# A hybrid attention and mLSTM layer on one core: log-sigmoid on token rows, attention stacks put together by DMA moves, two mLSTM evictions on ScalarE

## The chip, the cores and the metric

The kernel runs on one core of one Trainium2 chip. The metric is the time of one execution in microseconds on the device (us). In the profile PE is TensorE, PEld its weight loads, DVE is VectorE, ACT is ScalarE, POOL is GpSimd and SP is SyncE, whose work here is to issue DMAs. The engines run beside each other; each takes its own instructions strictly in the order in which the program lists them.

## The reference

One decoder layer over 1024 tokens of width 1024 in float32. The mixer projects the normalised input once and feeds two groups of heads, 8 attention heads of width 64 and 4 mLSTM heads of width 128; a gated feed-forward network with a short convolution follows.

```python
def _hybrid_mixer(h, w_in, ...):
    proj = h @ w_in
    aq, ak, av, mq, mk, mv, mo, mig, mfg = jnp.split(proj, SPLITS, axis=-1)
    att = _dilated_attention(att_heads(aq), att_heads(ak), att_heads(av))
    att = _rmsnorm(...)
    mqk = jax.nn.silu(_causal_dwconv(jnp.concatenate([mq, mk], axis=-1), mlstm_conv_w, mlstm_conv_b))
    ...
    log_i = (mig + mlstm_i_bias)
    log_f = jax.nn.log_sigmoid((mfg + mlstm_f_bias))
    hm = _mlstm_chunkwise(ml_heads(mq), ml_heads(mk) * (MLSTM_HEAD_DIM ** -0.5), ml_heads(mv), log_i, log_f)
    hm = jax.nn.sigmoid(mo) * _rmsnorm(...)
    return jnp.concatenate([att, hm], axis=-1) @ w_out

def _conv_ffn(h, w_ffn_up, ffn_conv_w, ffn_conv_b, w_ffn_down):
    gate, val = jnp.split(_causal_dwconv(h @ w_ffn_up, ffn_conv_w, ffn_conv_b), 2, axis=-1)
    return (jax.nn.silu(gate) * val) @ w_ffn_down
```

The attention scores are `q @ k.T`, 64 wide, over three dilated bands. In mLSTM the running sums of `log_f` and the running maxima over `log_f` and `log_i` give each token its weights.

## The kernel before

**Products in three parts.** A float32 operand is split into a rounded part and the rest (names with `h` and `l`: `xh`, `xl`, `w5h`, `w5l`), and a product is made of three matmuls of these parts (`mm3`, lines 315 to 318). ACT copies the first part, DVE or POOL subtracts it to get the second.

**The order.** Every stage is a generator, a lane with a priority. A planner (`Lanes.run`, lines 184 to 207) goes on with the first lane in order of priority whose tiles are ready by a model of the engines' clocks (`Clock`, lines 30 to 142). So the list of every engine is fixed when the program is built, and a change of one stage moves the instructions of others. Tiles of 128 x 1040 words are taken from 48 pages (`page`, `free`) and eight PSUM banks (`bank`, `freebank`); a lane that finds none free waits.

**The stages.** The projections run from the start to about 450 us in the order `m3 g0 g1 v0 m4 m5 v1 m6 m7 a0 h0 h1 h2 h3 a1 h4 h5 h6 h7` (line 392): `m` and `h` are the q and k rows of mLSTM and of attention heads, `g` the output gate with the eight i and f gate columns, `v` and `a` the values. Matmuls of mLSTM and attention are put between them. From about 450 us follow the output projection and, from about 625 us to the end, the feed-forward network, in which seven products take the place of eight by sums of blocks. These sums of weights are made by large DMAs from DRAM to DRAM (`sums`, lines 772 to 791): four pairs of a copy, issued by ACT, and an adding DMA, issued by POOL, of 5632 KB each into `usum` while the mixer runs, and later four pairs into `tsum`. All other DMAs are issued by SP, in one order, and SP waits in that order.

**The gates** (lines 696 to 767). `gn` holds the gate columns, 128 tokens x 8 tiles x 8. Sixteen transposes on PE turn them into rows `li` and `gz` of 4 x 1024, ACT evicts these with the bias; DVE and ACT make the log-sigmoid on the 4 x 1024 rows, DVE two scans, and from them `rows`, which PE transposes back (line 751) for all four mLSTM heads.

**mLSTM** (lines 794 to 890). For each half of a head four blocks: `ET` (decay weights), `ST` (weighted scores), `pk` (transposed k, multiplied by the last column of `ET`), and per block one PSUM bank with three products, whose first is copied to `nm` and whose second is added to it.

**Attention stacks** (lines 896 to 922). `t` holds q of one head on partitions 0 to 63 and k on 64 to 127. The scores need 128 partitions with both parts of both: `q1` is [first part; rest] and `q2` [rest; first part] of q, `kS` [rest; first part] of k. They are made by four copies and two subtractions of 64 partitions each, which move data between the halves as they go (in the trace `q` is both `q1` and `q2`). `copy` (lines 306 to 313) gives each copy to ACT or DVE, whichever is free first by the model.

Of the kernel before, what the change touches and what calls it, by code (L numbers as in the profile page):

```python
# [8 lines left out]
F32 = mybir.dt.float32  # L9
# [13 lines left out]
NBANK = 8  # L23
PGW = 1040

P_XN, P_FN, P_CW, P_CB, P_AW, P_MW, P_FW, P_FB, P_IB, P_FBI, P_N = (
    0, 8, 16, 48, 56, 60, 64, 64 + 132, 64 + 132 + 44, 64 + 132 + 45, 64 + 132 + 46)


class Clock:  # L30
# [187 lines left out]
def need(*tiles, pg=0, bk=0, cond=None, keep=0, kb=0):  # L218

    return tiles, pg, bk, cond, keep, kb  # L220
# [3 lines left out]
def tile_hybrid_layer(ctx, tc, xT, x, w_t, w_v, w_g, w_o, w_uq, w_dq, params, fnw, c_id, c_att, c_sel,  # L224
# [77 lines left out]

    def f32(ap):
        return ap.bitcast(F32)

    def copy(out_, in_, scale=None):

        if clk.eng.get("act", 0.0) <= clk.eng.get("dve", 0.0):
            act.activation(out_, in_, AF.Copy, **({} if scale is None else {"scale": scale}))
        elif scale is None:  # L310
            dve.tensor_copy(out_, in_)
        else:
            dve.tensor_scalar(out_, in_, scale, None, op0=OP.mult)
# [380 lines left out]
    G = {}  # L694

    def gates():
        yield need(pg=9, bk=1, cond=lambda: ("g", 1) in flags)
        rows_pg, urow_pg = page("rows"), page("urow", F32R)
        rows, urow = rows_pg[0:68, :S], urow_pg[0:64, :S]
        pool.memset(rows, 0.0)  # L700
        act.activation(urow, rows[0:64], AF.Copy)
        tmp = [page(n) for n in ("li", "gz", "lf", "ge", "gu", "gt", "uu")]
        li, z, lf, e, u, t, uu = [p[0:4, :S] for p in tmp]
        for hf in range(2):
            sl = slice(hf * 512, (hf + 1) * 512)
            for g, dst, b in ((0, li, P_IB), (1, z, P_FBI)):
                yield need(gn, bk=1)
                p = bank("pgt")
                for i in range(4):
                    pe.transpose(p[0:4, i * 128:(i + 1) * 128], gn[:, hf * 4 + i, g * 4:g * 4 + 4], ident)  # L710
                act.activation(dst[:, sl], p[0:4, :], AF.Identity, bias=pr[0:4, b:b + 1])
                freebank(p)
        yield need(z)
        dve.scalar_tensor_tensor(e, z, -1.0, z, op0=OP.mult, op1=OP.min)
        yield need(e)
        act.activation(e, e, AF.Exp)
        yield need(e)
        dve.tensor_scalar(u, e, 1.0, None, op0=OP.add)
        yield need(u)
        act.activation(lf, u, AF.Ln)  # L720
        dve.tensor_scalar(t, u, 1.0, None, op0=OP.subtract)
        dve.tensor_sub(t, e, t)
        dve.reciprocal(u, u)
        yield need(u)
        dve.tensor_mul(t, t, u)
        dve.tensor_add(lf, lf, t)
        dve.scalar_tensor_tensor(lf, z, 0.0, lf, op0=OP.min, op1=OP.subtract)
        yield need(lf)
        b, m = u, e
        dve.tensor_tensor_scan(b, rst, lf, 0.0, op0=OP.mult, op1=OP.add)  # L730
        dve.tensor_tensor_scan(m, lf, li, 0.0, op0=OP.add, op1=OP.max)
        yield need(m)
        dve.tensor_sub(uu, b, m)
        dve.tensor_sub(rows[0:4, :], li, b)
        yield need(rows)
        dve.tensor_scalar(rows[64:68, :], m, -41.0, None, op0=OP.max)
        act.activation(urow[0:4, :], uu, AF.Copy)
        dve.tensor_copy(rows[32:36, 0:128], uu[:, 0:128])
        u3 = uu.rearrange("p (c t) -> p c t", t=128)
        m3 = m.rearrange("p (c t) -> p c t", t=128)  # L740
        dve.tensor_tensor(rows[32:36, 128:].rearrange("p (c t) -> p c t", t=128), u3[:, 1:8, :],
                          m3[:, 0:7, 127:128].to_broadcast([4, 7, 128]), op=OP.add)
        dve.tensor_sub(urow[32:36, :], uu, f32(urow[0:4, :]))
        free(*tmp)
# [12 lines left out]
        yield need(rows, bk=1)
        p = bank("pdec")
        for h in range(4):
            pe.matmul(p[:, h * 8:(h + 1) * 8], sel[32:36, h * 128:(h + 1) * 128],  # L760
                      rows[32:36, 127:1024:128], start=True, stop=True)
        act.activation(dec.rearrange("p h c -> p (h c)"), p[:, :32], AF.Exp)
        freebank(p)
        free(rows_pg)
        G["urow"] = urow
        G["pg"] = urow_pg
        free(rst_pg, sel_pg)
# [26 lines left out]
    def mlstm(h):  # L794
# [8 lines left out]
        for hf in range(2):  # L803
# [27 lines left out]
                pe.transpose(pk[:, i * 128:(i + 1) * 128], k[:, c * 128:(c + 1) * 128], ident)  # L831
            yield need(pk)
            for i, c in enumerate(cs):
                dve.tensor_scalar(ET[:, 512 + i * 128:512 + (i + 1) * 128], pk[:, i * 128:(i + 1) * 128],
                                  ET[:, i * 128 + 127:i * 128 + 128], None, op0=OP.mult)
            freebank(pk)
            for i, c in enumerate(cs):
                yield need(ST, ET, *([Cp] if Cp is not None else []), bk=1)
                p = bank("pmc")
                o1, o2, o3 = p[:, 0:129], p[:, 129:258], p[:, 258:387]  # L840
                if c < 7:
                    pe.matmul(o3, ET[:, 512 + i * 128:512 + (i + 1) * 128], va[h][:, c, :], start=True, stop=True)
                pe.matmul(o1, ST[:, i * 128:(i + 1) * 128], va[h][:, c, :], start=True, stop=True)
                if c:
                    pe.matmul(o2, q[:, c * 128:(c + 1) * 128], Cp, start=True, stop=True)
                if c < 7:
                    Cn = small.tile([128, 129], F32, name="mC", bufs=4)
                    if c:
                        dve.scalar_tensor_tensor(Cn, Cp, dec[:, h, c:c + 1], o3, op0=OP.mult, op1=OP.add)
                    else:  # L850
                        dve.tensor_copy(Cn, o3)
                    Cp = Cn
                dve.tensor_copy(nm[:, c, :], o1)
                if c:
                    dve.scalar_tensor_tensor(nm[:, c, :], o2, icol[:, c, h:h + 1], nm[:, c, :],
                                             op0=OP.mult, op1=OP.add)
                freebank(p)
# [38 lines left out]
    def stacks(h, ps):  # L896
        for hf in range(2):
            yield need(pg=0 if hf else 4, keep=2, cond=lambda: fin_ready(ps, hf))
            if hf == 0:
                t = page("t")  # L900
            dve.tensor_mul(t[:, H[hf]], ps[hf], R[:, H[hf]])
            freebank(ps[hf])
        if h == 7:
            free(R)
        q1 = page("q1", F32R)
        q2 = page("q2", F32R)
        kS = page("kS", F32R)
        lo, up = slice(0, 64), slice(64, 128)
        A = slice(0, S)
        yield need(t)  # L910
        copy(q1[lo, A], t[lo, A])
        copy(kS[up, A], t[up, A])
        yield need(q1)
        dve.tensor_sub(q2[lo, A], t[lo, A], f32(q1[lo, A]))
        copy(q2[up, A], t[lo, A])
        yield need(kS)
        dve.tensor_sub(kS[lo, A], t[up, A], f32(kS[up, A]))
        yield need(q2)
        copy(q1[up, A], f32(q2[lo, A]))
        free(t)  # L920
        den = small.tile([128, 8], F32, name="aden", bufs=4)
        heads[h] = (q1, q2, kS, den)
# [699 lines left out]
def _lay_out(i):  # L1622
# [34 lines left out]
    p[:, P_MW:P_MW + 4] = a["mlstm_out_norm_w"][0].reshape(4, 128).T  # L1657
    p[:, P_FW:P_FW + 132] = a["ffn_conv_w"][0].reshape(3, 44, 128).transpose(2, 1, 0).reshape(128, 132)
    p[:, P_FB:P_FB + 44] = a["ffn_conv_b"][0].reshape(44, 128).T
    p[0:4, P_IB] = a["mlstm_i_bias"][0]  # L1660
    p[0:4, P_FBI] = a["mlstm_f_bias"][0]
    fnw = np.broadcast_to(a["final_norm_w"][None, :], (128, 1024))
    ident, att, sel, rst, tri = _consts()
    d = dict(xT=x.T, x=x, w_t=w_t, w_v=w_v, w_g=w_g, w_o=w_o, w_uq=w_uq, w_dq=w_dq, params=p, fnw=fnw,
# [19 lines left out]
```

## Time and profile before

| | us |
|---|---|
| median of 3 runs | 1235.93 |
| lowest and highest | 1235.52, 1237.56 |
| profiled execution, own time | 1236.24 |
| its span in the trace | 1234.4 |
| PE busy | 1216.6 |
| DVE busy | 899.7 |
| ACT busy | 590.3 |
| POOL busy | 300.2 |

1.84 us of the profiled execution lie outside the span. Times in the text are us from the start of the span. PEclk is the share of the full clock of 2.4 GHz that TensorE was granted; its other level is 1.2 GHz.

### The profile page before, as it was taken

What the parts mean: (1) busy time and instruction counts of PE and PEld (TensorE: products, weight loads), DVE (VectorE), ACT (ScalarE), POOL (GpSimd) and SP (SyncE); (2) the same over time, 40 slices, a digit from 0 to 9 for tenths busy, and PEclk for the clock granted to TensorE, in tenths of its full rate; (3) what the DMA queues carried; (4) which work ended last, traced back from release to release, by engine and by line L of the source; (5) the groups of instructions that cost most, each with busy time, mean ns of one, the idle gap of its engine ahead of it and who ended that gap; (6) DMA issues with size and microseconds to landing.
All of it is one profiled execution on the core that took longest, in us unless ns stands there. A gap on an engine that the chain in (4) does not pass through costs nothing.

```text
span 1234.4 us, 17447 instructions
## 1 busy us (share of the span) xinstructions
PE 1216.6 (99%) x6366; PEld 1027.3 (83%) x6366; DVE 899.7 (73%) x1692; ACT 590.3 (48%) x1108; POOL 300.2 (24%) x214
## 2 busy tenths in 40 slices
PE   8999999999999999999999999999999999999997
PEld 6899898988998888888778888888888888888886
DVE  6735875768876787535999878778687788877865
ACT  4464363347764775435654334334343444344553
POOL 3520212120302120501223222231222312324002
PEclk9999999999999999999999999999999999999999
DMA  9450847755192659344366567466524379432333
GB/s 329 182 190 18 192 140 250 162 145 184 56 203 68 224 221 226 116 157 129 103 217 177 190 247 180 154 208 177 178 87 152 105 299 408 132 100 92 101 95 145
DMA packets 63805, 208.01 MB, mean 169 GB/s; under 512 B 6756, under 2 KB 8292, under 8 KB 58728
## 3 DMA queue, kind: packets, MB, share of 16 engines
q1 hardware_dynamic: 58472, 137.69, 31.5%
q0 software_dynamic: 4352, 34.60, 13.8%
q10 hardware_dynamic: 896, 34.60, 8.5%
q8 instruction: 50, 0.82, 0.3%
q14 instruction: 35, 0.29, 0.1%
HBM read 182.76 MB, written 93.32 MB: 224 GB/s over the span
## 4 chain that ended last, share of the span: by engine, by line
PE 93%; DVE 3%; issue 2%; ACT 1%; POOL 1%; DMA 0%; SPq 0%; POOLq 0%; DVEq 0%
PE bank L153 93%; DVE gu L153 1%; DVE rows L153 0%; POOL w0l L153 0%; DVE xt L153 0%; DMA w0r<-in_w_t_dram 0%; DVE q L153 0%; ACT L153 0%; SPq L292 0%; DVE xb L153 0%; POOL rs L153 0%; DVE lf L153 0%; DVE ge L153 0%; ACT P L153 0%; ACT w1h L153 0%
## 5 line engine op out<-in xcount | busy, mean ns | idle before, releaser
L153 PE MATMUL bank<-xb,W 128*128 128x512 f32 x1848 | 431.6, 395 | 3.7 <-POOL W L153 2.0
L153 PEld LDWEIGHTS bank<-xb,W 128*128 128x128 f32 x1848 | 347.6, 188 | 86.6 <-POOL W L153 2.5
L153 PE MATMUL bank<-B,A 128*128 128x512 f32 x924 | 213.4, 393 | 0.0
L153 PEld LDWEIGHTS bank<-B,A 128*128 128x128 f32 x924 | 173.6, 188 | 39.7
L153 POOL TENSOR_TENSOR W<-ur,W 128x512 fp32r<-128x512 f32 x83 | 107.3, 1311 | 282.0 <-ACT W L153 272.2
L153 ACT ACTIVATE ua<-bank,pr 128x512 f32<-128x512 f32 x84 | 62.8, 776 | 163.2 <-DVE bank L153 153.8
L153 DVE SCALAR_TENSOR_TENSOR ua<-bank,pr,ua 128x511 f32<-128x511 f32 (+1 forms) x168 | 125.3, 746 | 15.9 <-ACT ua L153 12.9
L153 ACT ACTIVATE W<-ur 128x512 fp32r<-128x512 f32 x133 | 78.3, 623 | 18.6 <-DMA ur<-usum 18.0
L153 DVE TENSOR_TENSOR bank<-bank,ut 128x512 f32<-128x512 f32 x84 | 58.5, 696 | 34.1 <-PE bank L153 33.0
L153 ACT ACTIVATE A<-g 128x512 fp32r<-128x512 f32 x76 | 47.3, 626 | 70.6 <-DVE g L153 44.0
L153 DVE CUSTOM_DVE_ANT_0 P<-bank,matt 128x512 f32<-128x512 f32 (+3 forms) x96 | 50.5, 551 | 14.9 <-PE bank L153 14.7
L153 DVE TENSOR_TENSOR B<-br,B 128x512 fp32r<-128x512 f32 x67 | 50.4, 754 | 12.0 <-ACT B L153 11.9
L153 DVE TENSOR_TENSOR ut<-ut,bank 128x512 f32<-128x512 f32 x66 | 44.9, 681 | 19.4 <-PE bank L153 19.0
L153 ACT ACTIVATE P<-P,nmx 128x128 f32<-128x128 f32 (+3 forms) x64 | 49.4, 774 | 17.8 <-DVE nmx L153 16.7
L153 DVE TENSOR_TENSOR W<-ur,W 128x512 fp32r<-128x512 f32 x71 | 49.4, 701 | 8.8 <-ACT W L153 8.1
L153 POOL TENSOR_TENSOR A<-g,A 128x512 fp32r<-128x512 f32 x17 | 23.2, 1370 | 121.8 <-ACT A L153 121.7
L153 DVE TENSOR_TENSOR PT<-bank,PT 128x512 fp32r<-128x512 f32 (+1 forms) x80 | 47.6, 628 | 6.3 <-ACT PT L153 5.9
L153 DVE TENSOR_TENSOR A<-g,A 128x512 fp32r<-128x512 f32 x60 | 41.7, 699 | 14.2 <-ACT A L153 13.8
L153 ACT ACTIVATE B<-br 128x512 fp32r<-128x512 f32 x69 | 42.3, 619 | 16.1 <-DMA br<-in_w_dq_dram 10.5
L153 DVE TENSOR_TENSOR hq<-hq,bank 128x512 f32<-128x512 f32 x56 | 34.9, 679 | 20.5 <-PE bank L153 20.5
L153 PEld LDWEIGHTS bank<-PT,av 128*128 128x128 f32 x320 | 44.9, 192 | 3.8 <-DVE PT L153 1.5
L153 PE MATMUL bank<-PT,av 128*128 128x256 f32 (+1 forms) x320 | 47.0, 282 | 1.0 <-DVE PT L153 1.0
(358 smaller groups left out, 2491.7 us busy)
## 6 DMA issues: line engine op xcount, KB each, us to landing
usum<-in_w_uq_dram POOLq DMA_DIRECT2D x4, 5632.0 KB, 34.4
ur<-usum SPq DMA_DIRECT2D x88, 256.0 KB, 4.8
ur<-in_w_uq_dram SPq DMA_DIRECT2D x66, 256.0 KB, 4.5
usum<-in_w_uq_dram ACTq DMA_DIRECT2D x2, 5632.0 KB, 20.9
usum<-usum ACTq DMA_DIRECT2D x2, 5632.0 KB, 22.1
tsum<-in_w_dq_dram POOLq DMA_DIRECT2D x4, 2816.0 KB, 19.2
gp<-ua SPq DMA_DIRECT2D x22, 512.0 KB, 2.9
g<-gp SPq DMA_DIRECT2D x22, 512.0 KB, 7.6
```

Of the source, the lines that this page charges most:

```text
L153: r = f(*a, **k)
```

## The change

**Gates.** The bias and the whole log-sigmoid are computed on `gn`, token rows of 128 x 8 x 4, ahead of the sixteen transposes. The bias comes from a parameter tile in which it stands on every partition. What is transposed is the finished log_i and log_f; ACT evicts it with a plain copy. The lane asks for 7 pages in place of 9, and asks after the chain.

**mLSTM.** The four scaled evictions of `pk` per half head and the copy to `nm` per block are issued on ACT in place of DVE.

**Stacks.** One copy `q1` and one subtraction `q2` of all 128 partitions, and then four DMAs from SBUF to SBUF by SP, 64 x 1024 words (256 KB) each. The first two fill `kS` from the upper halves; the next two overwrite these upper halves with the lower half of the other tile, so the third waits until the second has landed and the fourth until the first has. `move` is new; its model takes 0.7 us of the queue and 2 us until landing.

```diff
+    def move(dst, src):
+
+        nc.sync.dma_start(f32(dst), f32(src))
+        t = max(clk.eng.get("dma", 1.7), clk.ready(src), clk.last(dst))
+        clk.eng["dma"] = t + 0.7
+        for a in (dst, src):
+            n = a.tensor.name
+            clk.acc[n] = max(clk.acc.get(n, 0.0), clk.eng["dma"] + 2.0)
...
     def gates():
-        yield need(pg=9, bk=1, cond=lambda: ("g", 1) in flags)
...
+        yield need(cond=lambda: ("g", 1) in flags)
+        yield need(gn)
+        gs = [small.tile([128, 8, 4], F32, name=f"g{n}", bufs=1) for n in "eult"]
+        e, u, l_, t = gs
+        z = gn[:, :, 4:8]
+        dve.tensor_tensor(gn, gn, pr[:, P_GB:P_GB + 8].unsqueeze(1).to_broadcast([128, 8, 8]), op=OP.add)
         dve.scalar_tensor_tensor(e, z, -1.0, z, op0=OP.mult, op1=OP.min)
...
+        dve.scalar_tensor_tensor(z, z, 0.0, l_, op0=OP.min, op1=OP.subtract)
+        yield need(gn, pg=7)
+        rows_pg, urow_pg = page("rows"), page("urow", F32R)
+        rows, urow = rows_pg[0:68, :S], urow_pg[0:64, :S]
+        pool.memset(rows, 0.0)
+        act.activation(urow, rows[0:64], AF.Copy)
...
+                act.activation(dst[:, sl], p[0:4, :], AF.Copy)
...
             for i, c in enumerate(cs):
-                dve.tensor_scalar(ET[:, 512 + i * 128:512 + (i + 1) * 128], pk[:, i * 128:(i + 1) * 128],
-                                  ET[:, i * 128 + 127:i * 128 + 128], None, op0=OP.mult)
+                act.activation(ET[:, 512 + i * 128:512 + (i + 1) * 128], pk[:, i * 128:(i + 1) * 128], AF.Copy,
+                               scale=ET[:, i * 128 + 127:i * 128 + 128])
...
-                dve.tensor_copy(nm[:, c, :], o1)
+                act.activation(nm[:, c, :], o1, AF.Copy)
...
+        yield need(t, pg=3)
         q1 = page("q1", F32R)
         q2 = page("q2", F32R)
         kS = page("kS", F32R)
         lo, up = slice(0, 64), slice(64, 128)
         A = slice(0, S)
-        yield need(t)
-        copy(q1[lo, A], t[lo, A])
-        copy(kS[up, A], t[up, A])
+        copy(q1[:, A], t[:, A])
         yield need(q1)
-        dve.tensor_sub(q2[lo, A], t[lo, A], f32(q1[lo, A]))
-        copy(q2[up, A], t[lo, A])
-        yield need(kS)
-        dve.tensor_sub(kS[lo, A], t[up, A], f32(kS[up, A]))
+        dve.tensor_sub(q2[:, A], t[:, A], f32(q1[:, A]))
         yield need(q2)
-        copy(q1[up, A], f32(q2[lo, A]))
+        move(kS[lo, A], q2[up, A])
+        move(kS[up, A], q1[up, A])
+        move(q1[up, A], q2[lo, A])
+        move(q2[up, A], q1[lo, A])
         free(t)
```

The change moves instructions on all engines from the gates to the output projection; from there PE's order is the same. Three places follow.

**The gates on DVE and PE.** DVE before, from the first instruction of the log-sigmoid to the last that writes `rows` for the transposes:

```order
L153 SCALAR_TENSOR_TENSOR ge<-gz 4x1024
L153 TENSOR_SCALAR gu<-ge 4x1024
L153 TENSOR_SCALAR gt<-gu 4x1024
L153 TENSOR_TENSOR gt<-ge,gt 4x1024
L153 RECIPROCAL gu<-gu 4x1024
L153 TENSOR_TENSOR gt<-gt,gu 4x1024
L153 TENSOR_TENSOR lf<-lf,gt 4x1024
L153 SCALAR_TENSOR_TENSOR lf<-gz,lf 4x1024
L153 SCALAR_TENSOR_TENSOR gu<-rst,lf 4x1024
L153 SCALAR_TENSOR_TENSOR ge<-lf,li 4x1024
L153 TENSOR_TENSOR uu<-gu,ge 4x1024
L153 TENSOR_TENSOR rows<-li,gu 4x1024
```

DVE now, up to the second scan:

```order
L153 TENSOR_TENSOR gn<-gn,pr 128x64
L153 SCALAR_TENSOR_TENSOR ge<-gn 128x32
L153 TENSOR_SCALAR gu<-ge 128x32
L153 TENSOR_SCALAR gt<-gu 128x32
L153 TENSOR_TENSOR gt<-ge,gt 128x32
L153 RECIPROCAL gu<-gu 128x32
L153 TENSOR_TENSOR gt<-gt,gu 128x32
L153 TENSOR_TENSOR gl<-gl,gt 128x32
L153 SCALAR_TENSOR_TENSOR gn<-gn,gl 128x8x4
L153 SCALAR_TENSOR_TENSOR gb<-rst,lf 4x1024
L153 SCALAR_TENSOR_TENSOR gm<-lf,li 4x1024
```

Nine short instructions on 128 partitions stand where eight long ones stood, and the scans follow. On PE the transposes of `gn` and those of `rows` stand as follows, before (the last matmuls ahead of `rows` are projections with `w4`):

```order
L153 MATMUL bank_101<-xh_124,w4h 128x512
L153 MATMUL bank_101<-xl_132,w4h 128x512
L153 MATMUL bank_101<-xh_124,w4l 128x512
L153 MATMUL bank_102<-ident,rows 128x68 x4
L153 MATMUL bank_95<-ident,rows 128x68 x4
L153 MATMUL bank_97<-rows,sel 128x8 x4
```

and now (they are still projections with `w3`):

```order
L153 MATMUL bank_97<-w3h,xh_124 128x256
L153 MATMUL bank_97<-w3l,xh_124 128x256
L153 MATMUL bank_97<-w3h,xl_132 128x256
L153 MATMUL bank_99<-ident,rows 128x68 x4
L153 MATMUL bank_100<-ident,rows 128x68 x4
L153 MATMUL bank_101<-rows,sel 128x8 x4
```

The sixteen transposes of `gn` stand 48 matmuls later than before, 72 matmuls of 128 x 256 stand between them and the transposes of `rows`, where 186 of 128 x 256 and 30 of 128 x 512 stood.

**Head 7's stack on DVE and SP.** DVE before, around its two subtractions (`PT` are transposed probabilities of head 6, `OT` the sum of its values, `ya` normalised attention):

```order
L153 TENSOR_TENSOR PT<-bank_95,PT 128x384
L153 TENSOR_TENSOR ya_4493<-ya_4493,adn 128x1024
L153 TENSOR_TENSOR q_4608<-t,q_4607 64x1024
L153 TENSOR_TENSOR kS<-t,kS 64x1024
L153 CAST PT<-bank_98 128x512
L153 CAST PT<-bank_96 128x384
L153 TENSOR_TENSOR OT<-bank_100,osum 64x256
L153 TENSOR_TENSOR PT<-bank_98,PT 128x512
L153 TENSOR_TENSOR PT<-bank_99,PT 128x512
```

DVE now, around the one that is left:

```order
L153 TENSOR_SCALAR nmx<-nmx 128x1
L153 TENSOR_TENSOR q_4573<-t,q_4572 128x1024
L153 TENSOR_TENSOR OT<-bank_102,osum 64x256
L153 TENSOR_TENSOR PT<-bank_99,PT 128x512
L153 TENSOR_TENSOR PT<-bank_95,PT 128x512
L153 TENSOR_TENSOR PT<-bank_97,PT 128x384
L153 TENSOR_TENSOR ya_4543<-ya_4543,adn 128x1024
L153 TENSOR_TENSOR PT<-bank_101,PT 128x512
```

The second subtraction and the two casts of `PT` no longer stand ahead of `OT`. SP now, with the four moves between loads of x (`h`); before, the loads follow each other:

```order
L292 DMA wr_4623<-in_w_o_dram 128x1024
L292 DMA wr_4625<-in_w_o_dram 128x1024
L292 DMA h_4627<-in_x_dram 128x1024
L292 DMA h_4645<-in_x_dram 128x1024
L308 DMA kS<-q_4573 64x1024
L308 DMA kS<-q_4572 64x1024
L308 DMA q_4572<-q_4573 64x1024
L308 DMA q_4573<-q_4572 64x1024
L292 DMA h_4708<-in_x_dram 128x1024
L292 DMA h_4742<-in_x_dram 128x1024
```

The moves stand behind two of eight loads and ahead of the other six. On PE, 45 output matmuls of 128 x 512, 14 matmuls of head 6's `PT` and 26 transposes lie between the last projection of head 7 and its first scores; before, 18, 4 and 24.

**The first mLSTM heads on ACT**, before:

```order
L153 ACTIVATE dec<-bank_97 128x32
L153 ACTIVATE ET<-ET,rcol 128x128 x8
L153 ACTIVATE w6h<-wr_1287 128x1024
L153 ACTIVATE w6h<-wr_1289 128x1024
L153 ACTIVATE mqk<-mz,pr 128x1024
L153 ACTIVATE ET<-ET,rcol 128x128 x4
L153 ACT_TABLE_LOAD
L153 ACTIVATE mqk<-mqk 128x1024
L153 ACT_TABLE_LOAD
L153 ACTIVATE ET<-ET,rcol 128x128 x4
```

and now:

```order
L153 ACTIVATE ET<-bank_97,ET 128x128 x4
L153 ACTIVATE ET<-bank_102,ET 128x128 x4
L153 ACTIVATE nm<-bank_98 128x129
L153 ACTIVATE nm<-bank_95 128x129
L153 ACTIVATE nm<-bank_96 128x129
L153 ACTIVATE nm<-bank_100 128x129
L153 ACTIVATE nm<-bank_101 128x129
L153 ACTIVATE nm<-bank_97 128x129
L153 ACTIVATE nm<-bank_98 128x129
L153 ACTIVATE ET<-ET,rcol 128x128 x4
```

The scaled evictions of `pk` (`ET<-bank,ET`) and the copies `nm<-bank` stand on ACT between the exponentials of `ET`.

## Rows read from the trace of the kernel before

**Rows 1.** The page, busy time of an engine, share of the span, instructions

```profile
PE 1216.6 (99%) x6366; PEld 1027.3 (83%) x6366; DVE 899.7 (73%) x1692; ACT 590.3 (48%) x1108; POOL 300.2 (24%) x214
```

**Rows 2.** Who waited for whom on PE: us in total, times, longest

```profile
PE bank L153 <- DVE OT L153: 2.1, 1, 2.1
PE bank L153 <- POOL W L153: 2.0, 1, 2.0
...
PE bank L153 <- DVE W L153: 1.1, 1, 1.1
...
PE bank L153 <- DVE rows L153: 0.6, 1, 0.6
```

**Rows 3.** Stretches of 30 us: busy time of each engine, PEclk, DMA share, GB/s

```profile
120.00:150.00 30.00, 29.42 (x188) 25.55 (x187) 25.98 (x45) 11.10 (x25) 8.73 (x4) 1.00 0.80 180
450.00:480.00 30.00, 26.66 (x149) 22.62 (x149) 25.93 (x67) 19.34 (x38) 9.80 (x5) 0.94 0.97 291
600.00:630.00 30.00, 26.31 (x103) 19.73 (x102) 29.23 (x46) 16.43 (x29) 8.67 (x6) 0.94 0.42 144
```

**Rows 4.** Instructions in order of time, 460 to 467: start, duration, instruction, idle

```profile
460.88 2.83 DVE L153 TENSOR_TENSOR q<-t,q 64x1024 fp32r<-64x1024 f32 x1 [0.50 <-ACT q L153]
...
463.74 1.22 DVE L153 TENSOR_TENSOR kS<-t,kS 64x1024 fp32r<-64x1024 f32 x1
...
464.88 1.14 DVE L153 CAST PT<-bank 128x512 fp32r<-128x512 f32 x2
466.05 0.42 DVE L153 TENSOR_TENSOR OT<-bank,osum 64x256 f32<-64x256 f32 x1
...
466.62 0.41 PE L153 MATMUL bank<-kS,q 128*128 128x128 f32 x2 [2.12 <-DVE OT L153]
```

**Rows 5.** The same, DVE, the gates

```profile
104.79 1.21 DVE L153 SCALAR_TENSOR_TENSOR ge<-gz 4x1024 f32<-4x1024 f32 x1 [27.12 <-ACT gz L153]
...
121.67 2.28 DVE L153 TENSOR_TENSOR_SCAN gu<-rst,lf 4x1024 f32<-4x1024 f32 x1
...
127.38 3.44 DVE L153 TENSOR_TENSOR rows<-li,gu 4x1024 f32<-4x1024 f32 x1
...
131.55 0.22 DVE L153 COPY rows<-uu 4x128 f32<-4x128 f32 x1
131.69 1.07 DVE L153 TENSOR_TENSOR rows<-uu,ge 4x896 f32<-4x896 f32 x1
```

**Rows 6.** The same, ACT, the gates

```profile
101.21 0.26 ACT L153 ACTIVATE gn<-bank,rn 128x8 f32<-128x8 f32 x1
...
106.08 1.28 ACT L153 ACT_TABLE_LOAD   x1
```

**Rows 7.** The same, PE, the gates

```profile
101.35 1.91 PE L153 MATMUL bank<-ident,gn 128*4 128x128 f32 x16
...
132.82 0.65 PE L153 MATMUL bank<-ident,rows 68*128 68x68 f32 x7 [0.58 <-DVE rows L153]
```

**Rows 8.** Groups of instructions on DVE, 100 to 300: count, busy us, mean ns

```profile
L153 DVE COPY nm<-bank 128x129 f32<-128x129 f32 x32 | 9.1, 285 | 0.4 <-PE bank L153 0.4
L153 DVE TENSOR_SCALAR ET<-bank,ET 128x128 f32<-128x128 f32 x32 | 9.0, 344 | 3.7 <-PE bank L153 3.7
```

**Rows 9.** The same, ACT

```profile
L153 ACT ACTIVATE va<-bank,rn 128x128 f32<-128x128 f32 x32 | 9.9, 361 | 18.8 <-PE bank L153 18.8
```

**Rows 10.** The same, DVE, 240 to 475

```profile
L153 DVE TENSOR_TENSOR q<-t,q 64x1024 fp32r<-64x1024 f32 x8 | 14.6, 1820 | 1.1 <-ACT q L153 0.9
```

**Rows 11.** DMA issues of the whole span: count, KB each, median us to landing

```profile
usum<-usum ACTq DMA_DIRECT2D x2, 5632.0 KB, 22.1
...
br<-tsum SPq DMA_DIRECT2D x44, 256.0 KB, 2.7
```

**Rows 12.** DMA of the tile wr, 300 to 320, one issue at 304.7

```profile
DMA to landing us min/median/max: 10.4/10.4/10.4
```

**Rows 13.** Instructions in order of time, 405 to 407, ACT queue

```profile
405.98 0.50 ACTq L783 DMA_DIRECT2D usum<-in_w_uq_dram  x1
```

More of the change, by code (lines that the diff above doesn't have):

```diff
@@ L24 @@
 PGW = 1040
-P_XN, P_FN, P_CW, P_CB, P_AW, P_MW, P_FW, P_FB, P_IB, P_FBI, P_N = (
-    0, 8, 16, 48, 56, 60, 64, 64 + 132, 64 + 132 + 44, 64 + 132 + 45, 64 + 132 + 46)
+P_XN, P_FN, P_CW, P_CB, P_AW, P_MW, P_FW, P_FB, P_GB, P_N = (
+    0, 8, 16, 48, 56, 60, 64, 64 + 132, 64 + 132 + 44, 64 + 132 + 52)
 class Clock:
@@ L304, in f32 @@
         return ap.bitcast(F32)
+    def move(dst, src):
[5 more added lines that the diff above has]
+            clk.acc[n] = max(clk.acc.get(n, 0.0), clk.eng["dma"] + 2.0)
+        for k in clk.cells(dst):
+            clk.wr[k] = clk.eng["dma"] + 2.0
+            clk.weng[k] = "dma"
     def copy(out_, in_, scale=None):
@@ L696, in gates @@
     def gates():
-        yield need(pg=9, bk=1, cond=lambda: ("g", 1) in flags)
[L698 to L713, printed above, removed]
+        yield need(cond=lambda: ("g", 1) in flags)
[4 more added lines that the diff above has]
+        dve.tensor_tensor(gn, gn, pr[:, P_GB:P_GB + 8].unsqueeze(1).to_broadcast([128, 8, 8]), op=OP.add)
         dve.scalar_tensor_tensor(e, z, -1.0, z, op0=OP.mult, op1=OP.min)
@@ L719, in gates @@
         yield need(u)
[L720 removed]
+        act.activation(l_, u, AF.Ln)
         dve.tensor_scalar(t, u, 1.0, None, op0=OP.subtract)
@@ L723, in gates @@
         dve.reciprocal(u, u)
-        yield need(u)
         dve.tensor_mul(t, t, u)
-        dve.tensor_add(lf, lf, t)
-        dve.scalar_tensor_tensor(lf, z, 0.0, lf, op0=OP.min, op1=OP.subtract)
+        yield need(l_)
+        dve.tensor_add(l_, l_, t)
+        dve.scalar_tensor_tensor(z, z, 0.0, l_, op0=OP.min, op1=OP.subtract)
[4 more added lines that the diff above has]
+        act.activation(urow, rows[0:64], AF.Copy)
+        tmp = [page(n) for n in ("li", "lf", "gb", "gm", "uu")]
+        li, lf, b, m, uu = [p[0:4, :S] for p in tmp]
+        for hf in range(2):
+            sl = slice(hf * 512, (hf + 1) * 512)
+            for g, dst in ((0, li), (1, lf)):
+                yield need(gn, bk=1)
+                p = bank("pgt")
+                for i in range(4):
+                    pe.transpose(p[0:4, i * 128:(i + 1) * 128], gn[:, hf * 4 + i, g * 4:g * 4 + 4], ident)
+                act.activation(dst[:, sl], p[0:4, :], AF.Copy)
+                freebank(p)
         yield need(lf)
-        b, m = u, e
         dve.tensor_tensor_scan(b, rst, lf, 0.0, op0=OP.mult, op1=OP.add)
@@ L1659, in _lay_out @@
     p[:, P_FB:P_FB + 44] = a["ffn_conv_b"][0].reshape(44, 128).T
-    p[0:4, P_IB] = a["mlstm_i_bias"][0]
-    p[0:4, P_FBI] = a["mlstm_f_bias"][0]
+    p[:, P_GB:P_GB + 4] = a["mlstm_i_bias"][0]
+    p[:, P_GB + 4:P_GB + 8] = a["mlstm_f_bias"][0]
     fnw = np.broadcast_to(a["final_norm_w"][None, :], (128, 1024))
```

## The prediction

> **What bounds the kernel now.** I read the page's busy times first: PE is busy 1216.6 of 1234.4 us [rows 1]. With no other engine near that, an edit on DVE or ACT moves the end only where PE waits, or where PE runs at the lower clock because it waited. The list of who PE waited for says where: 2.1 us once for `OT`, 2.0 and 1.1 us for weight splits `W`, 0.6 us once for `rows` [rows 2]. Then I cut the span into stretches of 30 us. Three hold what this change can touch [rows 3]: the gates (120 to 150), where PE is busy 29.42 us, so it loses 0.58; the end of attention (450 to 480), busy 26.66; and the start of the feed-forward network (600 to 630), busy 26.31. In the last two the granted clock is 0.94, and the reader should see both losses: 30 - 26.66 = 3.34 us of waiting, and 6% of 30 us = 1.8 us for running part of the stretch at 1.2 GHz, right after the wait. That makes 5.1 us at the end of attention, and 3.7 + 1.8 = 5.5 us at the feed-forward network. The instruction counts and shapes on PE don't change, so all else on PE stays.
>
> Why PE waits at 464 to 467 is in the instructions in order of time [rows 4]: PE's first scores of head 7 need the bank that the addition into `OT` reads. That addition runs at 466.05 because DVE has in front of it the two stack subtractions, 2.83 and 1.22 us, and two casts of `PT`, 1.14 us; PE idles 2.12 us until 466.62. This is a queue on DVE, not a matter of data.
>
> **Gates.** Removed: the log-sigmoid on 4 x 1024 rows takes DVE from 104.79 to the first scan at 121.67, 16.9 us [rows 5]. Added ahead of the transposes: nine DVE instructions of 32 to 64 columns. The nearest row is the copy of 128 columns, 0.22 us [rows 5], so nine take about 2.0; Exp and Ln, as long as the 8-column eviction of `gn`, 0.26 us each, and two table loads of 1.28 us [rows 6]; together 5.1 us after the last eviction of `gn` at 101.47, so 106.6. PE reaches the transposes of `gn` 48 matmuls later than before. The price of a matmul comes from PE itself: between the end of the transposes of `gn` and the wait for `rows` (103.26 to 132.24, 29.0 us, [rows 7]) it did 186 of 256 columns and 30 of 512, 62,976 columns, 0.46 ns a column. 48 of 256 columns are 5.7 us, so PE comes there at 101.35 + 5.7 = 107.0, and 106.6 is in time, by little.
>
> What follows is the path. Before, DVE's first instruction on the evicted rows starts 104.79 - 101.35 = 3.44 us after the first transpose [rows 5, 7]; keeping that, the first scan starts at 110.4 or so. From the first scan to the last write of `rows` it took 121.67 to 132.76, 11.1 us, in which one subtraction of 4 x 1024 took 3.44 where its like takes 1.21 [rows 5]; with 1.21 it is 8.9. So `rows` is ready at 119.3. PE has 72 matmuls of 256 columns after the transposes, 8.5 us: it comes at 107.0 + 1.9 + 8.5 = 117.4 and waits 1.9 us where it waited 0.6. **+1.3 us**, from -0.6 (`rows` ready in time) to +3.5 (the subtraction is again 3.44). The 16.9 us that DVE gets rid of are worth nothing: PE had 29 us of matmuls to run beside them, and now has 8.5. That cover is what the new order gives away.
>
> **mLSTM.** 32 evictions `ET` and 32 copies `nm` leave DVE, 9.0 + 9.1 = 18.1 us [rows 8]. The nearest ACT row is the scaled eviction of 128 x 128, 361 ns [rows 9]; 64 of them are 23 us on ACT. ACT is busy 11.10 us of 30 in the first mLSTM stretch and DVE 25.98 [rows 3], so there is room, and PE did not wait for DVE there but for `rows`. So nothing is gained; each block gets one more step from ACT to DVE, since the copy is now on another engine than the addition to it, hidden by projections. I take **+0.3 us**, from 0 to +2.
>
> ACT is dearer by the rows, 361 against 344 and 285 ns. The Trainium skill (ScalarE: Activation LUTs, Rules for kernel authors) says that multiplications and the like belong on VectorE and not on ScalarE; by itself that would make this part a loss of the 5 us that ACT takes more, but it counts only if ACT were on the path, and the busy times say that it is not.
>
> **Stacks.** Two subtractions of 64 partitions become one of 128, and four copies one; an instruction's time goes with its columns, so the subtraction that is left costs what one did, 1820 ns in the mean [rows 10]. At head 7 DVE loses the 1.22 us, and its two casts stand elsewhere, so the `OT` addition follows the one subtraction at once. Its wait of 2.12 us and the low clock behind it (1.8 us) go: at least 3.9 us. The rest of the 3.34 us is small waits for `PT` in the same queue; I take it all, **-5.1 us**, from -5.1 to 0 (if a new wait takes its place). At the other heads PE hardly waited, so nothing is gained there.
>
> What is late next? Each head's scores now wait for two rounds of moves, 32 moves in all. No DMA within SBUF is in the trace. The nearest row is 256 KB from DRAM, 2.7 us to landing [rows 11]; two rounds are 5.4 us, and the subtraction ends at 463.7 at the latest (its place in the queue before, [rows 4]), so head 7's moves land by 469.1. PE comes to these scores later than before: 27 more output matmuls of 512 columns lie ahead of them, 6.4 us by 0.46 ns a column, so at 464.5 + 6.4 = 470.9. Slack 1.8 us. SP's loads of `h` wait behind the moves for up to 5.4 us; DVE adds to them only later.
>
> **Sum.** 1236.24 - 5.1 + 1.3 + 0.3 = 1232.7 against the profiled execution, which stood 0.3 us above the median of its runs: **1232.4**.
>
> **Rivals.**
>
> *Head 7's wait only changes its name (no change).* If two moves of one round take turns, a round is 5.4 us and two are 10.8: landing at 474.5, PE waits 3.6 us and the low clock follows again. Then -5.1 becomes about 0: 1236.24 + 1.3 + 0.3 - 0.3, 1237.5; with 1.2 us of small waits gone it is about **1236**. Against it: a load of 512 KB took 10.4 us only beside a large copy, and nothing shows that a pair costs double. The Trainium skill (DMA: Bandwidth & Descriptors, Rules for kernel authors) says that two transfers to the two halves of the partitions serialise and advises one for all 128; no transfer here shows it.
>
> *A head's moves fall behind a large copy (slower).* The copies of 5632 KB take 22.1 us to land [rows 11], and a load that SP issued at 304.7, while one ran, took 10.4 us where 2.7 is usual for half its size [rows 12]. One such copy is issued at 405.98 [rows 13], about when head 5's moves are. It decides when the third and fourth move are issued after the copy has begun: they then land up to 22.1 us later. By its order PE has 87 matmuls of 34,560 columns between head 5's last projection and its first scores, 15.9 us; the multiplication, copy and subtraction of the stack and the first two moves take about 6 of them. So PE waits 22.1 - 9.9 = 12 us: **1244**. For it: planner and order know nothing of the copies' hold on the queues. Against it: all four moves need less than 6 us, so only a copy that begins in these holds them. The same with the adding DMA at head 7 would be +4 us.
>
> *The move brings more (faster).* The start of the feed-forward network loses 5.5 us, 2.0 of it for one `W` [rows 2]. Its order stays, but what comes before it shifts by some us against the DMAs that feed it. With that wait gone and half of the clock loss: 2.9 us more, **1229.5**. For it nothing speaks but the shift, and DVE is busy 29.23 of 30 us there [rows 3].
>
> **How the numbers follow.** Forecast 0.45, no change 0.22, slower 0.23, more 0.10. What the measurement can tell from no change is about 0.2%, 2.5 us. The forecast itself runs from 1230.2 (no longer wait at the gates, none on ACT) to 1235; some 0.07 of it lies within 2.5 us of the time before. So faster is 0.38 + 0.10 = 0.48, same 0.07 + 0.20 = 0.27, slower 0.25. The range goes from 1229 to 1243: 0.05 of the last rival lies below it, and above it 0.13, half of the slower one and a little of other ends.
>
> **What would show it.** PE busy in the stretch that ends attention rises from 26.7 to about 29.5 of 30 us at a clock of 1.00, with no wait for `OT`. PE's wait for `rows` is 1 to 4 us, near 117. Moves land within 3 to 4 us of their issue, except beside the large copies. The 600 to 630 stretch looks as before, shifted by 3 to 4 us. I am wrong if PE waits for `q` or `kS` by a DMA at any head, if the wait at the gates is gone, or if ACT shows up as releaser of PE between 118 and 260.

## The result, and the profile after

The changed kernel takes 1250.51 us (1249.37 to 1252.34), before 1235.72 us: 1.0121 times as long, 95% interval 1.0101 to 1.0141. That is 14.8 us slower, where 3.5 us faster was forecast, and above the range.

The page of the changed kernel, busy times, as [rows 1] of before:

```profile
PE 1221.0 (98%) x6366; PEld 1031.3 (83%) x6366; DVE 868.2 (69%) x1622; ACT 576.5 (46%) x1146; POOL 300.0 (24%) x213
```

The span is 14.9 us longer: PE is idle for 28.3 us in place of 17.8, and busy for 4.4 us more although it does the same matmuls. The list of who PE waited for (us in total, times, longest; [rows 2] of before):

```profile
PE bank L153 <- DMA q<-q: 10.9, 2, 8.9
PE bank L153 <- POOL W L153: 2.1, 1, 2.1
PE bank L153 <- DVE OT L153: 2.0, 1, 2.0
PE bank L153 <- DVE rows L153: 1.4, 2, 0.7
PE bank L153 <- ACT P L153: 1.3, 1, 1.3
```

The first row is new, 10.9 us for a DMA that writes `q`. The stretches of 30 us ([rows 3] of before; span of the stretch, busy times of PE, PEld, DVE, ACT, POOL, then PEclk, DMA share, GB/s) say where:

```profile
90.00:120.00 30.00, 28.60 (x243) 27.82 (x242) 12.01 (x19) 14.18 (x34) 0.00 (x0) 1.00 0.16 48
120.00:150.00 30.00, 30.00 (x204) 27.28 (x203) 10.20 (x24) 13.56 (x46) 3.60 (x2) 0.94 0.51 102
390.00:420.00 30.00, 28.84 (x153) 24.26 (x152) 17.97 (x49) 13.23 (x26) 7.33 (x4) 1.00 0.79 249
420.00:450.00 30.00, 20.26 (x109) 17.81 (x110) 14.56 (x43) 11.43 (x26) 0.00 (x0) 0.77 0.51 153
450.00:480.00 30.00, 28.73 (x189) 25.61 (x188) 25.95 (x67) 20.90 (x43) 8.13 (x3) 1.00 0.70 233
480.00:510.00 30.00, 29.50 (x180) 25.45 (x179) 20.25 (x55) 14.07 (x33) 1.69 (x3) 1.00 1.03 245
510.00:540.00 30.00, 28.03 (x141) 23.30 (x140) 17.68 (x29) 10.98 (x17) 7.64 (x3) 0.94 0.49 138
```

Four things are to be seen. At the gates PE waits 1.40 us in place of 0.58, and then has a clock of 0.94. At 390 to 450, where PE lost nothing before, it waits 1.16 + 9.74 us and has a clock of 0.77. At 450 to 480 it waits 1.27 us, where it lost 3.34 us and had a low clock. And at 510 to 540 it waits 1.97 us and has a low clock, where nothing was lost before. So the loss from 450 to 480 shrank, a much larger one came ahead of it and a smaller one behind it. The instructions in order of time, first PE and then the queues of SP and ACT (start, us, instruction, idle before and its releaser), show the large one:

```profile
427.74 0.48 PE L153 MATMUL bank<-kS,q 128*128 128x128 f32 x1 [8.89 <-DMA q<-q]
430.22 1.65 PE L153 MATMUL bank<-kS,q 128*128 128x128 f32 x5 [2.00 <-DMA q<-q]
```

```profile
397.80 1.10 SPq L308 DMA_DIRECT2D q<-q  x2
398.96 2.79 SPq L292 DMA_DIRECT2D wr<-in_w_o_dram  x4
403.54 1.11 SPq L308 DMA_DIRECT2D kS<-q  x2
411.53 1.10 SPq L308 DMA_DIRECT2D q<-q  x2
```

```profile
408.34 0.50 ACTq L799 DMA_DIRECT2D usum<-in_w_uq_dram  x1
```

These are head 5's scores. Its first two moves (403.54) stand on SP behind four loads of output weights, 512 KB each (398.96). From issue to landing they took, in the view of the tile `kS` for 403 to 405,

```profile
DMA to landing us min/median/max: 7.2/7.3/7.4
```

so that the last two, which wait for them, were issued at 411.53, 3.2 us after the copy of 5632 KB at 408.34. The one of these that is timed took, in the view of the tile `q` for 411 to 413,

```profile
DMA to landing us min/median/max: 16.2/16.2/16.2
```

and landed at 427.7, when PE's first scores begin; the other held the next ones until 430.22. Behind the waits PE works at 1.2 GHz, for 0.48 us from 427.74 and in this stretch (as [rows 3]):

```profile
430.22:435.10 4.88, 4.88 (x14) 4.11 (x15) 2.61 (x12) 0.49 (x2) 0.00 (x0) 0.50 0.14 58
```

That is 5.4 us of work at half the clock, so 2.7 us lost. The copy itself took, in the view of the tile `usum` for 408 to 409,

```profile
DMA to landing us min/median/max: 21.0/21.0/21.0
```

so it ended at 429.3. It did not stop the moves; it slowed them. The packets of the DMA queues from 412 to 426 (queue, packets, MB, share of the time of the 16 DMA engines; `q10` carries ACT's copy, `q1` what SP issued):

```profile
q10 hardware_dynamic: 104, 4.69, 94.2%
q1 hardware_dynamic: 76, 0.26, 5.3%
```

The copy's packets are 45 KB and take 2.0 us each (94.2% of 16 x 14 us, by 104); those of SP with data are 4 KB, 64 of them in 14 us. An estimate from these rows: if the two queues take turns by packet, the 128 packets of two moves, 8 for each of the 16 engines, stand behind 8 x 2.0 = 16 us of the copy, near the 16.2 measured.

The second new loss, at 513, on DVE and PE:

```profile
513.84 0.69 DVE L153 TENSOR_TENSOR h<-h,bank 128x512 f32<-128x512 f32 x1 [3.18 <-DMA h<-in_x_dram]
...
515.22 0.42 DVE L153 TENSOR_TENSOR OT<-bank,osum 64x256 f32<-64x256 f32 x1
```

```profile
515.69 0.44 PE L153 MATMUL bank<-ident,OT 128*128 128x128 f32 x2 [1.97 <-DVE OT L153]
```

DVE stands 3.18 us at an addition into `h` whose load has not landed, and the addition into `OT` that PE needs is queued behind it. The load is one of five that met the last adding DMA (issued at 480.39, 38.8 us to landing), in the view of the tile `h` for 480 to 502:

```profile
DMA to landing us min/median/max: 11.6/18.1/19.1
```

They do not wait for its end: they landed one after another at 493.0, 500.1, 506.9, 513.7 and 519.3, and it ended at 519.2. From 482 to 517 its packets (`q0`) were 8 KB and took 0.63 us each:

```profile
q0 software_dynamic: 695, 5.69, 78.6%
q1 hardware_dynamic: 823, 2.98, 24.1%
```

By the same estimate a load of 512 KB, 8 packets for each engine, takes 8 x (0.63 + 0.16) = 6.4 us beside it, near the 7 us from one landing to the next.

### The profile page after: what moved, and what is told of

Read it like the earlier page. It is cut to its first block, busy times and chain, and to the rows that moved or that the text cites. A ratio compares the mean times of both kernels' runs of the same rounds, so it can differ in the third digit from the quotient of the medians.

```text
span 1249.3 us, 17498 instructions
## 1 busy us (share of the span) xinstructions
PE 1221.0 (98%) x6366; PEld 1031.3 (83%) x6366; DVE 868.2 (69%) x1622; ACT 576.5 (46%) x1146; POOL 300.0 (24%) x213
## 3 DMA queue, kind: packets, MB, share of 16 engines
q0 software_dynamic: 4352, 34.60, 13.7%
## 5 line engine op out<-in xcount | busy, mean ns | idle before, releaser
L153 PE MATMUL bank<-kS,q 128*128 128x512 f32 (+3 forms) x192 | 42.4, 354 | 10.9 <-DMA q<-q 10.9
L153 ACT ACTIVATE B<-br 128x512 fp32r<-128x512 f32 x69 | 42.4, 619 | 14.9 <-DMA br<-in_w_dq_dram 10.1
L153 ACT ACTIVATE PT<-bank 128x512 fp32r<-128x512 f32 (+1 forms) x71 | 36.5, 547 | 24.9 <-PE bank L153 23.4
## 6 DMA issues: line engine op xcount, KB each, us to landing
tsum<-in_w_dq_dram POOLq DMA_DIRECT2D x4, 2816.0 KB, 18.1
```

Source lines behind the costliest of these rows:

```text
L153: r = f(*a, **k)
```

## The experiments

Theory A: both new losses have one cause. While a DMA of 5632 KB is under way, what SP issues lands late; head 5's last moves and the loads of `h` were issued into such DMAs. The rivals are told with each run.

**The last copy later.** The copy and its adding DMA are issued later; apart from them the lists of PE, DVE and ACT stay in the same order to 600 us.

```diff
-        for to, src, add in order:
+        for to, src, add, *later in order:
+            t += sum(later)
...
-                                      (3, (0, 1), 1), (7, (1, 0), 0), (7, (0, 0), 1))), 0.5)
+                                      (3, (0, 1), 1), (7, (1, 0), 0, 75), (7, (0, 0), 1, -20))), 0.5)
```

> The changed kernel with one thing moved: the copy of 5632 KB into the last sum block (the one issued at 408.3 us) is issued 75 us later by the plan, and its adding DMA 55 us later. Everything on PE, DVE and ACT up to the copy is in the same order. Theory A (head 5's last two moves stand behind this copy): they land 3 to 5 us after their issue at 411.5, ahead of head 5's scores at 418.5; PE's wait for them (8.9 + 2.0 us) and the low clock behind it go, 13.7 us in all: about 1236.8. Theory B (the moves are slow in themselves, 7 us a round as in head 5's first round): the second round lands at 419 to 420, PE still waits 1 to 3 us with a low clock behind: 1239 to 1241.

Measured: 1232.41 us, 0.9975 times before (0.9964 to 0.9986), 18.1 us less than the changed kernel. The last two moves were issued at 410.11, 1.4 us earlier than in the changed kernel and still after the time at which the copy stood there (408.34), and in the view of the tile `q` for 410 to 411.5 took

```profile
DMA to landing us min/median/max: 2.9/2.9/2.9
```

PE doesn't wait for `q` anywhere, nor for `OT`. Theory A holds, and the moves are not slow in themselves. The 18.1 us are more than the 13.7 expected, since the loss at 513 went too (the adding DMA was moved with the copy), and PE's clock did not fall at the gates. The first two moves still took 6.3 and 6.9 us, with no copy beside them, so it is the four loads of weights ahead of them that made these late. This run shows the gain that the prediction was after; its stretches at the gates and at the end of attention:

```profile
90.00:120.00 30.00, 28.60 (x245) 27.84 (x243) 11.81 (x18) 13.71 (x29) 0.00 (x0) 1.00 0.20 65
120.00:150.00 30.00, 30.00 (x213) 27.14 (x213) 10.75 (x27) 14.29 (x50) 3.62 (x2) 1.00 0.53 110
450.00:480.00 30.00, 28.73 (x176) 25.11 (x175) 23.43 (x60) 18.61 (x38) 8.63 (x4) 1.00 0.67 214
480.00:510.00 30.00, 30.00 (x182) 26.32 (x181) 25.36 (x48) 13.28 (x24) 6.36 (x3) 1.00 0.86 298
```

**Only the adding DMA later.** The copy stays at 408.

```diff
-                                      (3, (0, 1), 1), (7, (1, 0), 0), (7, (0, 0), 1))), 0.5)
+                                      (3, (0, 1), 1), (7, (1, 0), 0), (7, (0, 0), 1, 50))), 0.5)
```

> The changed kernel with only the last adding DMA (issued at 480.4 us by POOL) 50 us later; the copy at 408 stays. Theory: the loads of h, which took 11.6 to 19 us beside it, land in 3 to 6, DVE's additions into h no longer hold the queue, PE's wait for OT at 513 (2.0 us) and the low clock behind it go: 4 to 5 us less, 1245 to 1246.5, with head 5's wait of 8.9 and 2.0 us unchanged. Rival (the wait for OT comes from too few output matmuls left at the end, used up ahead of head 7's scores): it stays, 1249 to 1251.

Measured: 1246.56 us, 1.0097 times before (1.0082 to 1.0112), 4.0 us less than the changed kernel. Head 5's waits stay (9.0 and 2.2 us), the wait for `OT` is gone, and the five loads of `h` took, in the same view as above,

```profile
DMA to landing us min/median/max: 3.4/4.2/5.2
```

So the rival, that PE had used up its cover of output matmuls, falls. The two runs split the result. Between them lie 1246.56 - 1232.41 = 14.2 us. In the two profiles these are 11.2 us of waiting for `q`, and 3.1 us by which PE is busy longer (1218.1 against 1215.0), which is low clock. Of the latter 1.8 us fall on the gates, where this run's clock is 0.94 and the other's 1.00 from 120 to 150; only the remaining 1.3 stand behind head 5's waits. The loads of `h` are worth 4.0 us, and -3.1 us (1235.52 to 1232.41) is what the change does with both DMAs out of the way. These are differences between the same few times, so that their sum, +15.1, comes near the 14.8 measured is no test.

**Head 5 on the engines.** Only this head's stack is made by copies and subtractions.

```diff
+        if h == 5:
+            q1 = page("q1", F32R)
...
+            copy(q1[up, A], f32(q2[lo, A]))
+        else:
+            yield need(t, pg=3)
...
```

> The changed kernel with head 5's stack alone made by the four copies and two subtractions on ACT and DVE, as before the change; the other seven heads keep the moves. Theory A (only head 5's moves meet a copy at a bad time): the 13.7 us go, 1236 to 1238. Theory B (moves are too slow, head 5 only shows it first): head 6 or 7 waits next, by several us, 1240 or more.

Measured: 1241.73 us, 1.0050 times before (1.0035 to 1.0066). The time lies in the rival's range, but no head waits for a move, so theory A holds for the moves; 4 us more than expected remain. Its profiled execution loses 3.3 us to the clock at the gates (0.89 from 120 to 150). PE's longest wait is now for an addition into `h`, on DVE and in the list of PE's waits:

```profile
487.48 0.69 DVE L153 TENSOR_TENSOR h<-h,bank 128x512 f32<-128x512 f32 x1 [5.74 <-DMA h<-in_x_dram]
```

```profile
PE bank L153 <- DVE h L153: 3.9, 1, 3.9
```

It is the second loss again, larger.

**No moves.** The changed kernel with all stacks on the engines, as before the change (gates and evictions as changed; the edit puts the lines of `stacks` back).

> The changed kernel with all stacks as before the change; the gates on token rows and the two evictions on ACT stay. Theory A: the 13.7 us at head 5 go, the gates' loss of 2.6 us stays (1.4 us of waits for rows and a low clock after them), and the end of attention loses its 5 to 6 us as in both kernels: 1237 to 1239. Rival (the moves bring the 5 us at head 7 that were forecast, and the feed-forward start hides it): then the time is above that of the kernel whose copy comes later, by 3 us or more.

Measured: 1243.15 us, 1.0074 times before (1.0048 to 1.0100). The expectation is missed by 4 us. The time is 10.7 us above the run with the copy later, as the rival has it, but not for the rival's reason alone, since the end of attention was worse than in the kernel before:

```profile
PE bank L153 <- DVE ya L153: 3.3, 1, 3.3
PE bank L153 <- DVE nmx L153: 3.2, 1, 3.2
```

The next runs take this apart.

**The gates alone**, in the kernel before.

> The kernel before with the gates on token rows alone. Theory: only the waits at the gates grow, +1 to +2.5 us: 1237 to 1238. Rival (it is this part that made the kernel without moves lose 12.7 us at the end of attention): 1242 or more.

Measured: 1236.88 us, 1.0007 times before (0.9996 to 1.0018): at most what was expected. In its profile the wait for `rows` is 1.4 us as in the changed kernel, and the clock behind it 0.90 from 120 to 150.

**The evictions alone**, in the kernel before.

```diff
-                dve.tensor_scalar(ET[:, 512 + i * 128:512 + (i + 1) * 128], pk[:, i * 128:(i + 1) * 128],
-                                  ET[:, i * 128 + 127:i * 128 + 128], None, op0=OP.mult)
+                act.activation(ET[:, 512 + i * 128:512 + (i + 1) * 128], pk[:, i * 128:(i + 1) * 128], AF.Copy,
+                               scale=ET[:, i * 128 + 127:i * 128 + 128])
...
-                dve.tensor_copy(nm[:, c, :], o1)
+                act.activation(nm[:, c, :], o1, AF.Copy)
```

> The kernel before with the two mLSTM evictions on ACT alone. Theory: PE never waits for ACT between 118 and 260, and the shift of the order changes the end of attention by chance only: 1235 to 1238. Rival (it is this part that made the kernel without moves lose 12.7 us at the end of attention, by the other order): 1241 or more.

Measured: 1241.77 us, 1.0058 times before (1.0043 to 1.0073): the rival. But PE waits for nobody except `rows`, 0.6 us, from 118 to 262. The waits that are new are at the end of attention, the same two as without moves; besides, this execution loses 3.3 us to a clock of 0.89 from 120 to 150, behind the wait of 0.6 us. The wait for `ya`, on DVE:

```profile
507.48 0.69 DVE L153 TENSOR_TENSOR h<-h,bank 128x512 f32<-128x512 f32 x1 [4.29 <-DMA h<-in_x_dram]
...
509.40 1.22 DVE L153 TENSOR_TENSOR ya<-ya,adn 128x1024 f32<-128x1024 f32 x1
```

DVE stands 4.29 us at a load of `h` that the adding DMA slows down, ahead of the multiplication into `ya`.

**The evictions alone, and the adding DMA later** (both edits are shown above).

> The kernel before with the two evictions on ACT alone, and the last adding DMA 50 us later. Theory: its wait for ya at 507 (3.4 us) comes from loads of h that land at 502 to 509, as the adding DMA ends at 507; with that DMA later the loads land in time and the wait and its low clock go, 5 to 6 us less, 1236 to 1237; the wait for nmx near 459 (3.3 us) stays. Rival (ya waits because ACT, busier by the evictions, is late): it stays, 1241 or more.

Measured: 1236.62 us, 1.0013 times before (1.0003 to 1.0023), 5.2 us less. The wait for `ya` is gone, that for `nmx` stays (3.3 us; it stands in the place of the waits for `OT` and `PT` of the kernel before). So with that DMA out of the way the evictions cost 0.4 to 2.8 us by the interval; the rest of their loss was the new order, which put the loads of `h` at a worse time against the adding DMA. The kernel before with that DMA alone later was not run, so what is theirs of the 0.4 to 2.8 us isn't shown.

**The moves alone**, in the kernel before: `stacks` and `move` as in the change.

> The kernel before with the stacks by moves alone; gates and evictions as before the change. On SP the loads of the output weights and head 5's moves stand in the same order as in the changed kernel. Theory A: the same meeting of copy and moves costs 10 to 14 us, the gates' 2.6 us are saved: 1245 to 1249. Rival (it is the ACT load of the evictions that makes the moves late): the copy is met by no move and the time is within 3 us of the kernel before.

Measured: 1265.53 us, 1.0241 times before (1.0222 to 1.0259). Head 5 meets the copy as in the changed kernel, and head 3 meets the adding DMA that POOL issues at 337.05:

```profile
360.07 0.45 PE L153 MATMUL bank<-kS,q 128*128 128x128 f32 x1 [8.51 <-DMA q<-q]
363.70 0.47 PE L153 MATMUL bank<-kS,q 128*128 128x128 f32 x1 [3.19 <-DMA q<-q]
```

```profile
437.71 0.48 PE L153 MATMUL bank<-kS,q 128*128 128x128 f32 x1 [8.10 <-DMA q<-q]
440.98 1.33 PE L153 MATMUL bank<-kS,q 128*128 128x128 f32 x4 [2.79 <-DMA q<-q]
```

Twice the same loss, 11.7 and 10.9 us of waiting with the clock behind each. The order of the whole kernel decides which head it is. The expectation had only head 5; head 3's moves were issued at 338.25, 1.2 us after that DMA.

**Head 5's moves ahead of the loads.** The loads of the output weights are let go only once head 5's moves are issued; both large DMAs stay.

```diff
-                flags.add("late")
+                flags.add("h6")
...
         move(q2[up, A], q1[lo, A])
+        if h == 5:
+            flags.add("late")
```

> The changed kernel with the six loads of output weights issued after head 5's moves in place of before them; both large DMAs stay. Theory: without four loads of 512 KB ahead of them, head 5's first two moves land in 3 to 4 us in place of 7.2 to 7.4, the last two are issued near 407, a microsecond before the copy, and land in 3 to 4 us: the wait goes, 1236 to 1238, the wait by the loads of h stays. Rival (a move in flight is held as well once the copy begins): they land near 428 and the wait of 9 us stays, 1249 or more.

Measured: 1268.23 us, 1.0277 times before (1.0260 to 1.0294). The mechanism was right and the time wrong by 31 us. Head 5's last moves were issued at 406.48 and 407.04, the copy at 407.82, and they took

```profile
DMA to landing us min/median/max: 2.9/3.3/3.7
```

So a move that is issued 0.8 us ahead of the copy is not held. But the six loads of weights, the first of them issued at 407.65, 0.2 us ahead of the copy, and the others behind it, now meet it, and took

```profile
DMA to landing us min/median/max: 20.8/21.8/24.0
```

ACT waits for the first of them ahead of its exponentials `P`, and PE for these; and head 7's moves, issued at 473, meet the adding DMA of 472.02 and take 7.9 to 12.6 us each:

```profile
428.85 1.06 ACT L153 ACTIVATE w0h<-wr 128x1024 fp32r<-128x1024 f32 x1 [14.92 <-DMA wr<-in_w_o_dram]
```

```profile
435.05 0.90 PE L153 MATMUL bank<-ident,P 128*128 128x128 f32 x3 [15.38 <-ACT P L153]
```

```profile
494.44 0.44 PE L153 MATMUL bank<-kS,q 128*128 128x128 f32 x1 [8.54 <-DMA q<-q]
```

**The kernel before with the last copy later**, the control for the first run: the same edit of `sums`.

> The control: the kernel before the change with the last 5632 KB copy and its adding DMA later, exactly as in the run with the copy later. Theory A (the loss at the end of attention was the queue on DVE with the stack's two subtractions): nothing changes, PE still waits 2 us for OT near 464 and the time is 1235 to 1236. Rival (the loss came from the adding DMA at 462.6, which held the loads of h): the loss of 5 to 6 us goes here too, 1230 to 1231, and the moves have no part in the gain.

Measured: 1239.56 us, 1.0031 times before (1.0017 to 1.0044). The wait for `OT` of 2.1 us stays, and a wait for `ya` of 3.1 us is new, since the copy at 480.76 now slows down three loads of `h`, 20.0 to 21.5 us. So the later copy by itself gains nothing; the gain of the first run comes with the change, and the wait for `OT`, which stays here, is gone there. The moves alone with the copy later were not run. The expected "nothing changes" missed the loads of `h` a third time.

**The later copy and the gates as before**: moves and evictions as changed.

> The kernel with moves, evictions on ACT and the copy later, but with the gates as before the change. Theory: the gates cost 1.4 us of waits for rows and up to 1.7 us of low clock (the run with the copy later lost 2.0 + 0.6 us from 90 to 150, the kernel before 0.7), so this is 1 to 2 us faster than that run: 1230 to 1231.5. Rival (shorter work on DVE at the gates speeds later stages): slower than that run, 1233 or more.

Measured: 1229.51 us, 0.9955 times before (0.9940 to 0.9970): faster than both kernels, by 6.0 and 21.0 us. It is 2.9 us under the run with the changed gates. The wait for `rows` is 0.6 us in place of 1.4; 1.0 us less is waited for weight splits `W` from DVE and ACT at the start of the feed-forward network (0.5 in place of 1.1 and 0.4), whose order the change doesn't touch, and why isn't settled.

## Why the prediction was wrong

*What bounds the kernel* was read rightly: all differences are waits of PE and low clock behind them.

*Gates, +1.3 us.* The wait came at 117.31 and 118.22, 1.40 us in all, where 1.9 us at 117.4 were worked out. Against 0.58 that is +0.8. What the term left out is the clock: PE falls to 1.2 GHz after the wait in the changed kernel's profile (0.94 from 120 to 150, 1.8 us) and not in that of the run with the copy later (1.00), after the same 1.40 us. It also falls with the old gates, after 0.6 us, in the kernel before with the evictions alone (0.89) and with the copy later (0.94), and not in the kernel before itself (1.00). So this loss is not the change's alone, and what decides it stays open.

*mLSTM, +0.3 us.* ACT released PE nowhere between 118 and 262. The evictions alone, with the loads of `h` out of the way, measured 1.0013 (1.0003 to 1.0023): 0.4 to 2.8 us, 1.6 in the middle, more than the 0.3 taken and within its bounds of 0 to +2. The Trainium skill (ScalarE: Activation LUTs, Rules for kernel authors) advises VectorE and not ScalarE for multiplications; the 5 us of ACT time that this would have cost do not show, as PE does not wait for ACT there.

*Stacks, -5.1 us.* The queue on DVE was the cause of the wait at 464, and the moves remove it: in the run with the copy later 450 to 480 loses 1.27 us at a clock of 1.00, where it lost 3.34 and 1.8. That is -3.9, the "at least" that was named, and not the -5.1 taken; the 1.27 us are a wait for `P` on ACT and not for `PT`. Of a pair of moves the first takes 2.9 us to landing and the second 3.6 (head 6's in the run with the copy later), and as the second is issued 0.6 us after the first, a round takes 4.2 us where 2.7 was taken. All four take 8.3 us there, 427.88 to 436.2, and not 5.4. The rival that a pair takes turns had 5.4 for a round and 10.8 for two, so the truth lies between; the wait that it priced at head 7 did not come, since PE came to these scores at 473.04 and the last move had landed at 469.2. The Trainium skill (DMA: Bandwidth & Descriptors, Rules for kernel authors) says that transfers to the two halves serialise; here the second lands 1.3 us after the first, and its time is not doubled.

That the run with the copy later measures the forecast's 1232.4 is in part luck: -3.9 and +0.8 stand there in place of -5.1 and +1.3.

*The step that failed* is the question what is late next, and in it two sentences. "All four moves need less than 6 us, so only a copy that begins in these holds them": the first two took 7.2 to 7.4 us, because four loads of 512 KB stood ahead of them on SP, and so the last two were issued 3.2 us after the copy. Without such loads the first two took 2.9 and 3.6 us (head 5's moves ahead of the loads), and the last two were then issued ahead of the copy and not held. The order of SP that would have shown the loads ahead of head 5 was not worked into the price; and four moves need 8.3 us on an empty queue, too. And "SP's loads of `h` wait behind the moves for up to 5.4 us; DVE adds to them only later": the addition stands on DVE ahead of `OT`, and the adding DMA, which the prediction did not set against these loads, made them take 11.6 to 19.1 us. The sign of being wrong that the prediction named first, a wait for `q` by a DMA, came at head 5 with 10.9 us.

*The rival "a head's moves fall behind a large copy"* had mechanism, head and copy right, with 0.23, and 1244. Its price for the wait, 12 us, was measured as 10.9. Left out were the low clock behind the wait (2.7 us), the one at the gates (1.8 us) and the loads of `h` (4.0 us): 1244 - 1.1 + 2.7 + 1.8 + 4.0 = 1251.4, near the measured 1250.5.

## What to carry to other kernels

Before a step is put on the DMA queue, list every large transfer of the program with its start and end, and what stands ahead of the step on its own queue at that time; then price it by the latest of these and not by an empty queue. A chain of two rounds of DMAs is decided by the issue of its second round. Where an order is planned by a model that knows nothing of the large transfers, any change of order can move a small load into one, and the loss then shows far from the edit.

## What the runs showed of the hardware

A transfer of 256 KB within SBUF that was issued 0.8 us ahead of a DMA of 5632 KB on another queue landed in 3.7 us at most; issued 3.2 us after it, it took 16.2 us and landed 1.6 us before the large one's end. A load of 512 KB that was issued 0.2 us ahead of such a DMA took 20.8 us. Neither large DMA stopped the small ones: beside the copy, in packets of 45 KB (2.0 us each), SP's queue moved 64 packets of 4 KB in 14 us, and beside the adding DMA, in packets of 8 KB (0.63 us each), a load of 512 KB landed every 7 us or so. Both counts fit queues that take turns by packet, so that the size of the large DMA's packets sets how slow the small ones get; but no run changed that size.

After waits of 8.9 and 2.0 us PE's clock was 0.77 over the stretch from 420 to 450, against 0.94 from 510 to 540 after a wait of 2.0 us.
